# A hybrid attention block: the gate of GLA's second head before the second pair's queries and keys, its temporaries in other places, and pools of attention that wait tile by tile

## The chip, the cores and the metric

The kernel runs on one core of a Trainium2 chip, in one launch. The metric is the device time of one execution in microseconds (us). The kernel before takes 1225.82 us, the median of three runs (1225.39 to 1226.3).

## The reference

One encoder block over 1024 tokens (a grid of 16 rows and 64 columns) of width 1024, in float32. One normed input feeds one projection whose columns go to two kinds of attention heads: 8 heads of neighbourhood attention with a bias table, and 4 heads of gated linear attention (GLA), which is scanned in chunks of 64 tokens in both directions.

```python
n = rmsnorm(h, ln_g)
proj = n @ w_in
qa, ka, va, qg, kg, vg, rg, zf, zb = jnp.split(proj, offsets, axis=-1)
y_na = neighbourhood_attention(na_heads(qa), na_heads(ka), na_heads(va), rpb)
y_gla = bidirectional_gla(qg, kg, vg, rg, zf, zb, gu_f, gb_f, gu_b, gb_b, norm_g)
h = h + jnp.concatenate([y_na, y_gla], axis=-1) @ w_out
h = h + jnp.square(jax.nn.relu(rmsnorm(h, ln_ff_g) @ w_ff1)) @ w_ff2
return rmsnorm(h, ln_final_g)
```

Within GLA, per head and direction, with decay gates `log_a` from the low-rank factors z:

```python
b = jnp.cumsum(log_a.reshape(B, H, N, C, dk), axis=-2)
q_dec = q * jnp.exp(b)
k_inv = k * jnp.exp(-b)
A = jnp.where(mask, jnp.einsum('bhnid,bhnjd->bhnij', q_dec, k_inv), 0.0)
o_intra = jnp.einsum('bhnij,bhnje->bhnie', A, v)
contrib = jnp.einsum('bhncd,bhnce->bhnde', k * jnp.exp(b_last - b), v)
...
o = rmsnorm(o, norm_g) * jax.nn.silu(r)
```

## The kernel before

The work goes through stages: the x stage (load, norm, low-rank factors z, queries and keys of the first pair of heads; until about 44 us), GLA (to about 275), neighbourhood attention (to about 460), the output projection, the feed-forward part, and the final norm. The change touches the first three.

**Projections.** A projection takes one block of 128 columns of `w_in`. Float32 accuracy comes from two-part products: the normed input is kept as high and low part (nh, nl), the weights as wh and wl, and each of 8 steps along the width takes three matmuls (`product`, L198), so half a block (512 tokens) is 24 matmuls of 128x512. `proj` (L248) does two such halves, each into a PSUM buffer of the tag "mm", which has two: a half can start only when the half two before has been read out by its evacuation. The first stage's z sums use the same tag.

**Weights.** `weights` (L163) loads a block (wf, from SyncE's queue), makes wl by an ACT pass (L172) and a DMA of GpSimd that adds the block (L173), and wh by an ACT cast (L175). These ACT passes keep their program order. Two buffers of each: wf for the next block but one is sent for when wh of the block before is cast. The blocks follow the list `BLOCKS` (L48).

**Order of the work.** TensorE's instructions run in program order. On the other engines a scheduler orders them by priority, in which place in the program counts and `tc.high_priority(offset=...)` moves instructions up; each engine then works its list through strictly in order. GLA's own steps leave TensorE time, which generators fill: `Fill` (L122) steps through the projections of `FILL_ORDER` (L46): "v" values, "r" output gates, "q" queries and keys of the second pair of heads, "n" and "k" the first queries and keys of neighbourhood attention.

**Evacuations.** `qk_evac` (L267) scales half a projection of a pair of heads: for each of the two heads VectorE writes 64 rows (L278) and ACT copies them to the other 64 (L279). `z_evac` (L337) reads the z sums on VectorE (zf, L340), casts on ACT (zT, L341) and subtracts on VectorE (L342). `rstd_from` (L214) turns sums of squares to rms by Ln, Exp, Identity, Square on ACT and two VectorE passes; its temporaries are nt, nu and ny. `gla_v` (L449) reads values, `gla_r` (L466) an output gate: VectorE scales it (rm, L473), ACT takes Abs, Exp, Ln and Exp (L474 to L478), and VectorE finishes. Its temporaries rt and rm lie in the tags "g0" and "g1" of the pool "gla", two buffers each, which the norm of GLA, the decay gates (`gla_gates`, L497) and the values' temporaries use as well.

**GLA's steps for one head.** `gla_keys` (L519) forms kD, kI and qD; `gla_ktok` (L540) transposes kD (kt); `gla_contrib` (L555) sums states, ACT copies them (st, L568 and L571); `gla_scan` (L587) runs them through; `gla_within` (L573) makes the scores a, which VectorE masks into asb (L584); `gla_norm` (L611) norms and multiplies with yg (L617, L618).

**Start of attention.** The pools "na" and "qkv" open at L713 on memory that GLA's tiles had; a pool opened so waits until everything in that memory is done. Then the mask is loaded by GpSimd's queue (msk, L731) and the bias table of the first pair of heads by SyncE's (bt, L737); VectorE completes bt with msk (L742), and the softmax of the first block of scores sc reads it (L797).

Of the kernel before, what the change touches and what calls it, by code (L numbers as in the profile page):

```python
# [10 lines left out]
F32 = mybir.dt.float32  # L11
F32R = mybir.dt.float32r
U32 = mybir.dt.uint32
AF = mybir.ActivationFunctionType
ALU = mybir.AluOpType
# [3 lines left out]
P = 128  # L19
D = 1024  # L20
T = 1024
H = 512
# [22 lines left out]
)  # L45
FILL_ORDER = (('v', 0), ('r', 0), ('v', 1), ('q', 1), ('r', 1), ('v', 2), ('v', 3), ('r', 3), ('r', 2), ('n', 0), ('k', 0))  # L46

BLOCKS = (4, 8, 5, 1, 3, 9, 6, 7, 11, 10, 12, 16, 20, 13, 17, 21, 14, 18, 22, 15, 19, 23)  # L48
SOON = 200
SOON_W = 100  # L50
SOON_O = 100
SOON_V = 50
# [13 lines left out]
def block_kernel(ctx, tc, xT, g_mix, w_in, w_z, rpb, na_mask, gu, gb, g_gla, sel_f, sel_b,  # L66
                 rst, w_out, g_ff, w1, w2, g_fin, out):
    nc = tc.nc
    V, S, DMA, G = nc.vector, nc.scalar, nc.sync, nc.gpsimd

    L = "left"
    R = "right"
    pool = lambda name, side, bufs=1: tc.tile_pool(name=name, bufs=bufs, side=side)
# [89 lines left out]
    def weights(block, eng=None):  # L163


        with tc.high_priority(offset=SOON_W):
            wf = stg.tile([P, D], F32, tag="wf", name="wf")
            DMA.dma_start(wf, block)
            if eng is not None:
                return split(wf, eng)  # L170
            wl = stg.tile([P, D], F32R, tag="wl", name="wl")
            tc.keep_in_program_order(S.activation(wl, wf, AF.Copy, scale=-1.0))  # L172
            G.dma_start(wl, block, accum_op=ALU.add)  # L173
            wh = stg.tile([P, D], F32R, tag="wh", name="wh")
            tc.keep_in_program_order(S.copy(wh, wf))  # L175
            return wh, wl
# [3 lines left out]
    def block_parts(blk):  # L180

        if not parts:
            parts[blk] = weights(w_in[blk], G)
        n = BLOCKS.index(blk) + 1
        if n < len(BLOCKS):
            parts[BLOCKS[n]] = weights(w_in[BLOCKS[n]])
        return parts.pop(blk)
# [54 lines left out]
    rms = n_p.tile([P, T], F32, tag="rms", name="rms")  # L242
# [5 lines left out]
    def proj(blk, evac):  # L248

        w = block_parts(blk)  # L250
        for hf in range(2):
            d = bank("mm", f"proj{blk}_{hf}")
            yield from proj_part(d, w, hf * H, H)
            evac(hf, d)
# [5 lines left out]
    g0 = gla_stack.enter_context(pool("gla0", R))  # L260
# [6 lines left out]
    def qk_evac(g, which):  # L267

        dic, sc, t = ((qd, 0.125, "q"), (kd, 1.0, "k"))[which]
        for i in range(2):  # L270
            dic[2 * g + i] = (g0 if t == "q" and i else gk).tile([P, T], F32, tag={"k0": "k00", "q0": "k10", "k1": "k20"}.get(f"{t}{i}", "qd1"), name=f"{t}d{2*g+i}")

        def ev(hf, d):
            c = slice(hf * H, (hf + 1) * H)
            for i in range(2):
                dst = dic[2 * g + i]
                a, b = (slice(0, 64), slice(64, 128))[::1 - 2 * i]
                V.scalar_tensor_tensor(dst[a, c], d[a, :], sc, rms[a, c], op0=ALU.mult, op1=ALU.mult)  # L278
                S.copy(dst[b, c], dst[a, c])  # L279
        return ev  # L280

# [116 lines left out]
    def perm(t, hf):  # L398
        return t.rearrange("p (b r c) -> p b r c", b=NB, r=ROWS)[:, :, hf * 8:(hf + 1) * 8, :]

    def nat(d):
        return d.rearrange("p (r b c) -> p b r c", r=8, b=NB)

    def na_proj(p, nm, parts, tmp):

        def ev(hf, d):
            t = tmp()
            with tc.high_priority(offset=SOON):  # L410
                V.tensor_tensor(t, d, rms[:, hf * H:(hf + 1) * H], op=ALU.mult)
            x = [perm(x, hf) for x in parts]
            for i in range(2):
                own, other = slice(i * 64, i * 64 + 64), slice(64 - i * 64, 128 - i * 64)
                ti, hi = nat(t[own, :]), x[i][own]
                S.copy(hi, ti)
                if nm == "k":
                    S.copy(x[i][other], ti)
                lo, eng = (x[2][own], V) if nm == "k" else (x[i][other], G)
                eng.tensor_tensor(lo, ti, hi.bitcast(F32), op=ALU.subtract)  # L420
        return proj({"q": 12, "k": 16}[nm] + p, ev)


    yn_p = yg_pool.enter_context(pool("yn", L))
    q0 = [yn_p.tile([P, T], F32R, tag=f"yn{2 + i}", name=f"q0{i}") for i in range(2)]

# [17 lines left out]
    with pool("gla", R) as gp:  # L444
# [4 lines left out]
        def gla_v(h):  # L449
# [3 lines left out]
            def ev(hf, d):  # L453
                tmp = gp.tile([P, H], F32, tag="g1", name="vtmp", bufs=2)
                with tc.high_priority(offset=SOON):
                    V.tensor_tensor(tmp, d, rms[:, hf * H:(hf + 1) * H], op=ALU.mult)
# [9 lines left out]
        def gla_r(h):  # L466

            def ev(hf, d):
                c = slice(hf * H, (hf + 1) * H)
                t = gp.tile([P, H], F32, tag="g0", name="rt", bufs=2)  # L470
                m = gp.tile([P, H], F32, tag="g1", name="rm", bufs=2)
                with tc.high_priority(offset=SOON):
                    V.tensor_tensor(m, d, rms[:, c], op=ALU.mult)  # L473
                S.activation(t, m, AF.Abs)  # L474
                S.activation(t, t, AF.Exp, scale=-1.0)
                S.activation(t, t, AF.Ln, bias=1.0)
                V.scalar_tensor_tensor(t, m, 0.0, t, op0=ALU.min, op1=ALU.subtract)
                S.activation(t, t, AF.Exp)  # L478
                dst = t if (h, hf) in normed else yg[h][:, c]
                V.scalar_tensor_tensor(dst, m, ggla[:, 0:1], t, op0=ALU.mult, op1=ALU.mult)  # L480
                if (h, hf) in normed:
                    V.tensor_tensor(yg[h][:, c], yg[h][:, c], t, op=ALU.mult)
                else:
                    gated.add((h, hf))
            return proj(8 + h, ev)
# [137 lines left out]
                yield from proj(blk, qk_evac(g, which))  # L623

        def first_q(_):
            return na_proj(0, "q", q0, lambda: gp.tile([P, H], F32, tag="g1", name="qt", bufs=2))

        def first_k(_):

# [5 lines left out]

        for kind, i in FILL_ORDER:
            gen = {"v": gla_v, "r": gla_r, "q": gla_qk, "n": first_q, "k": first_k}[kind](i)
            fill.add(gen, (kind, i))
# [40 lines left out]
    yn = [yn_q.tile([P, T], F32, tag=f"yn{h}", name=f"yn{h}") for h in range(2)]  # L679
# [30 lines left out]
        with tc.high_priority(offset=SOON_O):  # L710
            V.tensor_tensor(hT[:, d, c], hT[:, d, c], o, op=ALU.add)

    with pool("na", L) as ap, pool("qkv", L) as qp:  # L713


        ap.tile([P, 2, 3], F32, tag="sm", name="sm", bufs=4)
        msk, bt0, pt0 = None, None, {}
        for tag in ("pt00", "pt01", "x", "msk", "pt10", "pad", "bt", "pt11", "vhl"):
            if tag == "msk":
                msk = ap.tile([P, 4, P], F32, tag="msk", name="msk")  # L720
# [7 lines left out]
                vhl[0] = ap.tile([P, NB, 2, P], F32R, tag="vhl", name="vhl0")  # L728
            else:
                pt0[tag] = ap.tile([P, 3, 3, P], F32R, tag=tag, name=f"pt0{tag[2:]}")  # L730
        G.dma_start(msk, na_mask)  # L731

        def bias_for(p):


            bt = bt0 if p == 0 else ap.tile([P, 2, 7, P], F32, tag="bt", name=f"bt{p}")
            DMA.dma_start(bt[:, :, 0:3, :], rpb2[:, 2 * p:2 * p + 2, :, :])  # L737
            rows = msk[:, 3:4, :].to_broadcast([P, 2, P])
            for i in range(2):
                for o, src, m in ((3, 1, rows), (5, 0, rows), (0, 0, msk[:, 0:3, :])):  # L740
                    n = 3 if o == 0 else 2
                    V.scalar_tensor_tensor(bt[:, i, o:o + n, :], bt[:, i, src:src + n, :], 8.0, m,  # L742
                                           op0=ALU.mult, op1=ALU.add)
            return bt
# [7 lines left out]
        def na_v(p):  # L752
# [18 lines left out]
            def ev(hf, d):  # L771

                if not hf:
                    vT.append((gk if p % 2 else qp).tile([P, T], F32, tag=f"k2{1 - p % 2}", name=f"vT{p}"))
                with tc.high_priority(offset=SOON):
                    V.tensor_tensor(perm(vT[0], hf), nat(d), nat(rms[:, hf * H:(hf + 1) * H]), op=ALU.mult)
# [85 lines left out]
        qt = lambda: qp.tile([P, H], F32, tag="qt", name="qt", bufs=2)  # L862
        qk = qk_tiles(0)
        fill.add(na_v(0), ("v", 0))
        bt = bias_for(0)
        fill.run(NA_PRE)
        xs = softmax(0, 0, *qk, bt)
        for p in range(NH // 2):
# [11 lines left out]
            for b in range(NB):  # L880
# [5 lines left out]
                if b + 1 == NB and p + 1 < NH // 2:  # L886
                    fill.until(("k", p + 1))
                    qk, bt = nxt, bias_for(p + 1)
# [68 lines left out]
    for d in range(NK):  # L957
        o = bank(("t", "s", "o")[d % 3], f"opl_{d}")
        t = yhl[0][:, NK - 1]
# [327 lines left out]
    with tc.high_priority(offset=150):  # L1287
        for n in range(2):
            p, i = f1.order[n]
# [131 lines left out]
    for c0, n in ((H, H), (0, Q), (Q, Q)):  # L1421
        c = slice(c0, c0 + n)
# [108 lines left out]
```

## Time and profile before

| | |
|---|---|
| median of three runs | 1225.82 us |
| the profiled execution | 1222.21 us |
| its span, first to last instruction | 1220.4 us |
| granted TensorE clock, mean | 0.982 of full |
| busy: TensorE matmul, VectorE, ACT, GpSimd | 1162.6, 873.1, 665.8, 248.1 us |
| longest waits of TensorE | 9.0 us at 275.61, 5.0 us at 103.34, 3.7 us at 243.39, 3.3 us at 219.28 |

The profile is of one execution, 3.6 us shorter than the median of the runs. In its rows, a timeline row gives start and duration in us, engine, line of the kernel, operation, output and inputs with their shapes, a count, and in brackets the idle time ahead and what ended it. A row of waits gives who waited and for which instruction: total, times, longest. PE is TensorE, DVE is VectorE, POOL is GpSimd, SP is SyncE, and SPq its queue of DMA issues. L113 is the helper through which every matmul goes, so matmuls are told apart by their tiles. Equal rows that follow each other are put together, with the count behind the x.

### The profile page before, as it was taken

To read this page: it belongs to the slowest core of one execution; us is meant where nothing else is said; L and a number is where in the kernel's file an instruction comes from. 1 tells how busy PE (TensorE), PEld (TensorE's weight loads), DVE (VectorE), ACT (ScalarE), POOL (GpSimd) and SP (SyncE) were. 2 spreads that over 40 slices of the span, in tenths; PEclk is the share of its full clock that TensorE was granted. 3 is DMA by queue.
4 is the path that set the end of the run, shared out by engine and by line. 5 is a ranking of instruction groups with operands and counts; after the bars stand their busy time and mean duration, and the time that the engine had idled before them with its cause. 6 is when DMAs were issued, how large, how long until landed. Compare 5 with 4: busy or idle time off the path is not lost.

```text
span 1220.4 us, 15431 instructions
## 1 busy us (share of the span) xinstructions
PE 1162.6 (95%) x5632; PEld 952.0 (78%) x5632; DVE 873.1 (72%) x1558; ACT 665.8 (55%) x1222; POOL 248.1 (20%) x199
## 2 busy tenths in 40 slices
PE   8998899886999999998999999999999999999996
PEld 8876687664877878876778888888888888888775
DVE  8786768645768686575776885876858768587467
ACT  6756565743656675443643644536445364453664
POOL 5200000201111213441103140321403214032004
PEclk9999899998999999998999999999999999999998
DMA  7333131313223314330111211112111121111203
GB/s 232 80 93 78 35 70 35 69 35 91 51 67 83 70 59 178 104 137 1 40 64 35 70 53 52 52 53 70 52 54 51 52 69 52 56 49 52 70 1 138
DMA packets 40283, 84.03 MB, mean 69 GB/s; under 512 B 9264, under 2 KB 20656, under 8 KB 40208
## 3 DMA queue, kind: packets, MB, share of 16 engines
q1 hardware_dynamic: 36608, 71.11, 17.5%
q0 software_dynamic: 3456, 11.94, 5.6%
q8 instruction: 44, 0.72, 0.2%
q14 instruction: 31, 0.25, 0.1%
q10 hardware_dynamic: 144, 0.00, 0.0%
HBM read 78.85 MB, written 5.96 MB: 69 GB/s over the span
## 4 chain that ended last, share of the span: by engine, by line
PE 72%; DVE 15%; ACT 8%; issue 2%; DMA 1%; SPq 0%; POOL 0%; DVEq 0%; ACTq 0%
PE f L113 24%; PE u L113 21%; PE proj L113 12%; PE op L113 5%; PE sc L113 2%; PE no L113 2%; DVE st L592 1%; PE pt L118 1%; PE o L113 1%; DVE st L589 1%; DMA bt<-rpb 1%; DVE nf L934 1%; DVE pl L1004 1%; DVE asb L584 1%; PE ob L113 1%
## 5 line engine op out<-in xcount | busy, mean ns | idle before, releaser
L1026 ACT CAST ph<-A 128x512 fp32r<-128x512 f32 x166 | 103.0, 621 | 146.2 <-PE f L113 73.3
L1004 POOL TENSOR_TENSOR ul<-uB,uh 128x512 fp32r<-128x512 f32 x84 | 109.1, 1317 | 330.5 <-ACT uh L1039 216.3
L113 PE MATMUL proj<-nh,wh 128*128 128x512 f32 x352 | 152.3, 433 | 8.3 <-DVE qd L278 5.0
L113 PE MATMUL f<-uh,ph 128*128 128x512 f32 x400 | 155.9, 390 | 1.6 <-ACT u L1047 1.4
L113 PE MATMUL f<-ul,ph 128*128 128x512 f32 x400 | 155.7, 389 | 0.1
L113 PE MATMUL f<-uh,pl 128*128 128x512 f32 x400 | 155.7, 389 | 0.0
L1004 DVE TENSOR_TENSOR pl<-A,ph 128x512 fp32r<-128x512 f32 x166 | 112.7, 688 | 52.6 <-ACT ph L1026 52.6
L113 PE MATMUL proj<-nh,wl 128*128 128x512 f32 x352 | 140.1, 398 | 0.0
L113 PE MATMUL proj<-nl,wh 128*128 128x512 f32 x352 | 139.4, 396 | 0.0
L1186 DVE TENSOR_TENSOR hT<-hT,f 128x512 f32<-128x512 f32 x168 | 113.0, 686 | 19.9 <-PE f L113 19.9
L113 PE MATMUL u<-n,ph 128*128 128x512 f32 x288 | 90.2, 395 | 2.0 <-ACT ph L939 2.0
L113 PEld LDWEIGHTS f<-uh,ph 128*128 128x128 f32 x400 | 75.1, 188 | 17.9 <-ACT u L1047 1.8
L113 PEld LDWEIGHTS proj<-nh,wh 128*128 128x128 f32 x352 | 67.6, 192 | 27.4 <-issue 14.7
L113 PEld LDWEIGHTS f<-ul,ph 128*128 128x128 f32 x400 | 75.1, 188 | 16.0 <-DVE ul L1004 0.4
L113 PEld LDWEIGHTS f<-uh,pl 128*128 128x128 f32 x400 | 75.1, 188 | 15.6
L1039 ACT CAST uh<-uB 128x512 fp32r<-128x512 f32 x84 | 51.9, 618 | 51.3 <-PE f L113 34.5
L113 PE MATMUL u<-T,ph 128*128 128x512 f32 x256 | 79.2, 391 | 0.1
L113 PEld LDWEIGHTS proj<-nh,wl 128*128 128x128 f32 x352 | 67.1, 191 | 15.3
L113 PE MATMUL op<-y,wh 128*128 128x512 f32 x240 | 77.0, 402 | 0.4 <-DVE y L693 0.4
L113 PEld LDWEIGHTS proj<-nl,wh 128*128 128x128 f32 x352 | 67.9, 193 | 11.9 <-issue 1.7
L173 POOL DMA_DIRECT2D wl<-in_w_in x21 | 18.1, 864 | 257.9 <-ACT wl L172 223.7
L799 ACT ACTIVATE xsc<-xsc,sm 128x384 f32<-128x384 f32 (+1 forms) x64 | 37.3, 584 | 58.5 <-DVE sm L797 58.0
(300 smaller groups left out, 2557.1 us busy)
## 6 DMA issues: line engine op xcount, KB each, us to landing
A<-in_w SPq DMA_DIRECT2D x64, 512.0 KB
wf<-in_w_in SPq DMA_DIRECT2D x22, 512.0 KB
wl<-in_w_in POOLq DMA_DIRECT2D x21, 512.0 KB, 6.9
wf<-in_w_out SPq DMA_DIRECT2D x17, 512.0 KB
hT<-in_xT SPq DMA_DIRECT2D x2, 2048.0 KB
xs<-in_xT SPq DMA_DIRECT2D x6, 512.0 KB
out<-hT SPq DMA_DIRECT2D x4, 512.0 KB
out<-hT SPq DMA_DIRECT2D x8, 256.0 KB
```

The lines of the kernel that those rows point to most:

```text
L113: m = nc.tensor.matmul(*args, **kw)
L118: tc.keep_in_program_order(nc.tensor.transpose(*args, **kw))
L173: G.dma_start(wl, block, accum_op=ALU.add)
L584: V.copy_predicated(asb[hf], sel.bitcast(U32).to_broadcast([P, 4, P]), src.rearrange("p (a b) -> p a b", a=4))
L589: V.scalar_tensor_tensor(st[0:64, i + 1, :], st[0:64, i, :], dec[0:64, i:i + 1], st[0:64, i + 1, :], op0=ALU.mult, op1=ALU.add)
L592: V.scalar_tensor_tensor(st[64:128, j - 1, :], st[64:128, j, :], dec[64:128, j:j + 1], st[64:128, j - 1, :], op0=ALU.mult, op1=ALU.add)
L799: S.activation(x[:, :n], x[:, :n], AF.Exp, scale=-1.0, bias=sm[:, i, 0:1], accum_out=sm[:, i, 1:2])
L934: V.scalar_tensor_tensor(dst, hT[:, d, hf * H:(hf + 1) * H], gff[:, d:d + 1], r, op0=ALU.mult, op1=ALU.mult)
L1004: return kp(eng.tensor_tensor(l, x, h.bitcast(F32), op=ALU.subtract))
L1026: kp(S.copy(ph, x))
L1039: kp(S.copy(uh, x))
L1186: kp(V.tensor_tensor(hT[:, d, c], hT[:, d, c], o[:, s], op=ALU.add))
```

## The change

It has four parts. The output gate of the second head (r1, block 9) moves ahead of the queries and keys of the second pair (blocks 1 and 3), in the fill order and in the list of weights. The VectorE half of `qk_evac` gets a raised priority, for both pairs. The gate's two temporaries become one tile rtm, in the two places yn2 and yn3, one for each half; these are the places of the first attention queries q0, which are therefore allocated later, in the generator that makes them. And the pools "na" and "qkv" wait tile by tile for the memory that they take over, while the mask's load and the first bias table get a raised priority.

```diff
-FILL_ORDER = (('v', 0), ('r', 0), ('v', 1), ('q', 1), ('r', 1), ('v', 2), ('v', 3), ('r', 3), ('r', 2), ('n', 0), ('k', 0))
+FILL_ORDER = (('v', 0), ('r', 0), ('v', 1), ('r', 1), ('q', 1), ('v', 2), ('v', 3), ('r', 3), ('r', 2), ('n', 0), ('k', 0))
-BLOCKS = (4, 8, 5, 1, 3, 9, 6, 7, 11, 10, 12, 16, 20, 13, 17, 21, 14, 18, 22, 15, 19, 23)
+BLOCKS = (4, 8, 5, 9, 1, 3, 6, 7, 11, 10, 12, 16, 20, 13, 17, 21, 14, 18, 22, 15, 19, 23)
 SOON = 200
+SOON_B = 300
...
-                V.scalar_tensor_tensor(dst[a, c], d[a, :], sc, rms[a, c], op0=ALU.mult, op1=ALU.mult)
+                with tc.high_priority(offset=SOON):
+                    V.scalar_tensor_tensor(dst[a, c], d[a, :], sc, rms[a, c], op0=ALU.mult, op1=ALU.mult)
                 S.copy(dst[b, c], dst[a, c])
...
-    q0 = [yn_p.tile([P, T], F32R, tag=f"yn{2 + i}", name=f"q0{i}") for i in range(2)]
+    q0 = []
...
-                t = gp.tile([P, H], F32, tag="g0", name="rt", bufs=2)
-                m = gp.tile([P, H], F32, tag="g1", name="rm", bufs=2)
+                tm = yn_p.tile([P, 2, H], F32, tag=f"yn{2 + hf}", name="rtm")
+                t, m = tm[:, 0, :], tm[:, 1, :]
...
         def first_q(_):
-            return na_proj(0, "q", q0, lambda: gp.tile([P, H], F32, tag="g1", name="qt", bufs=2))
+            q0.extend(yn_p.tile([P, T], F32R, tag=f"yn{2 + i}", name=f"q0{i}") for i in range(2))
+            yield from na_proj(0, "q", q0, lambda: gp.tile([P, H], F32, tag="g1", name="qt", bufs=2))
...
-    with pool("na", L) as ap, pool("qkv", L) as qp:
+    soon = lambda name: tc.tile_pool(name=name, bufs=1, side=L, reuse_waits="tile")
+    with soon("na") as ap, soon("qkv") as qp:
...
-        G.dma_start(msk, na_mask)
+        with tc.high_priority(offset=SOON_B):
+            G.dma_start(msk, na_mask)
...
-        bt = bias_for(0)
+        with tc.high_priority(offset=SOON_B):
+            bt = bias_for(0)
```

Lines after the edits are numbered one to six higher than before. VectorE's order at the end of the x stage, before; `z_354` are the z sums of the second half, `sb` and `ob` the sums of the first pair's queries and keys:

```order
L228 TENSOR_TENSOR nt<-nt,nu 128x256
L229 SCALAR_TENSOR_TENSOR rms<-nt,rms 128x256
L340 TENSOR_TENSOR zf<-z_354,rms 64x512
L278 SCALAR_TENSOR_TENSOR qd_157<-sb_371,rms 64x512
L278 SCALAR_TENSOR_TENSOR qd_158<-sb_371,rms 64x512
L342 TENSOR_TENSOR zT<-zf,zT 64x512
L278 SCALAR_TENSOR_TENSOR kd_159<-ob_528,rms 64x512
L278 SCALAR_TENSOR_TENSOR kd_160<-ob_528,rms 64x512
```

And after:

```order
L229 TENSOR_TENSOR nt<-nt,nu 128x256
L230 SCALAR_TENSOR_TENSOR rms<-nt,rms 128x256
L280 SCALAR_TENSOR_TENSOR qd_157<-sb_371,rms 64x512
L280 SCALAR_TENSOR_TENSOR qd_158<-sb_371,rms 64x512
L280 SCALAR_TENSOR_TENSOR kd_159<-ob_528,rms 64x512
L280 SCALAR_TENSOR_TENSOR kd_160<-ob_528,rms 64x512
L342 TENSOR_TENSOR zf<-z_354,rms 64x512
L344 TENSOR_TENSOR zT<-zf,zT 64x512
```

All four evacuations of the first pair stand ahead of zf now. On ACT at the same place, before (wl and wh are the passes over the next block's weights; rms, nt those of the last quarter's norm):

```order
L219 ACTIVATE nt<-ssq,small 128x256
L226 ACTIVATE nu<-ssq,small 128x256
L220 ACTIVATE rms<-nt,small 128x256
L227 ACTIVATE nt<-rms 128x256
L172 ACTIVATE wl<-wf 128x1024
L175 CAST wh<-wf 128x1024
L341 CAST zT<-zf 64x512
```

And after:

```order
L220 ACTIVATE nt<-ssq,small 128x256
L227 ACTIVATE nu<-ssq,small 128x256
L173 ACTIVATE wl<-wf 128x1024
L176 CAST wh<-wf 128x1024
L221 ACTIVATE rms<-nt,small 128x256
L228 ACTIVATE nt<-rms 128x256
L281 COPY qd_157<-qd_157 64x512
```

The weight passes stand ahead of the norm's Exp and Square now. VectorE in GLA, where the second head's keys are formed, before; `proj_0_970` and `proj_1_1047` are the two halves of the second pair's queries:

```order
L531 TENSOR_TENSOR kD_1152<-kD_1152,kd_160 128x1024
L278 SCALAR_TENSOR_TENSOR qd_961<-proj_1_1047,rms 64x512
L537 TENSOR_TENSOR qD_1161<-qD_1161,qd_158 128x1024
L278 SCALAR_TENSOR_TENSOR qd_962<-proj_0_970,rms 64x512
L278 SCALAR_TENSOR_TENSOR qd_962<-proj_1_1047,rms 64x512
```

And after, where `proj_1_1045` is the second half of gate r1 and `proj_0_1102` the first half of the queries:

```order
L482 SCALAR_TENSOR_TENSOR yg_101<-rtm,ggla 128x512
L537 TENSOR_TENSOR kI_1164<-kI_1164,kd_160 128x1024
L475 TENSOR_TENSOR rtm<-proj_1_1045,rms 128x512
L533 TENSOR_TENSOR kD_1154<-kD_1154,kd_160 128x1024
L539 TENSOR_TENSOR qD_1163<-qD_1163,qd_158 128x1024
L479 SCALAR_TENSOR_TENSOR rtm<-rtm 128x512
L482 SCALAR_TENSOR_TENSOR yg_101<-rtm,ggla 128x512
L280 SCALAR_TENSOR_TENSOR qd_1093<-proj_0_1102,rms 64x512
```

The gate's one pass has come ahead of kD and qD, and the queries' passes behind both. On SyncE's queue the first bias table stands behind the same loads of weights as before; the last of them is the one that goes out at 274.32.

## The prediction

> **What bounds the kernel now.** I read the engine line of the page first, then the list of what TensorE waited for, then the timelines of the engines around its three longest waits.
>
> ```profile
> PE 1162.6 (95%) x5632; PEld 952.0 (78%) x5632; DVE 873.1 (72%) x1558; ACT 665.8 (55%) x1222; POOL 248.1 (20%) x199
> ...
> PE sc L113 <- DVE sm L797: 9.0, 1, 9.0
> PE proj L113 <- DVE qd L278: 5.0, 1, 5.0
> PE a L113 <- DVE asb L584: 4.8, 3, 3.7
> PE proj L113 <- DVE rm L473: 3.3, 1, 3.3
> ```
>
> TensorE is busy for 95% of the span, and the change alters none of its matmuls, so only its idle time and its clock can move. The four rows under the page's line are its longest waits before the output projection (total, times, longest). Three of the four meet the change: 9.0 us ahead of the first attention scores, 5.0 us ahead of the key projection of the second pair, 3.3 us ahead of the first attention queries. The third (asb) stays as it is: the masks, the scan and what GpSimd does beside it are untouched.
>
> A long wait costs more than itself. This is the table of stretches; the column with a value between 0.5 and 1, behind the five busy times, is the granted clock:
>
> ```profile
> 108.00:113.00 5.00, 4.66 (x21) 4.12 (x22) 0.80 (x2) 3.22 (x4) 0.85 (x1) 0.66 0.17 24
> 224.00:229.00 5.00, 5.00 (x27) 4.05 (x26) 3.85 (x6) 4.97 (x9) 0.00 (x0) 1.00 0.01 3
> 247.00:252.00 5.00, 4.26 (x21) 3.50 (x22) 2.92 (x6) 0.00 (x0) 0.00 (x0) 0.66 0.71 150
> ```
>
> Behind the waits of 5.0 and 3.7 us the clock is 0.66 over 5 us, which loses 0.34 x 5 = 1.7 us of TensorE work; behind the 3.3 us it is 1.00 and nothing is lost.
>
> **Term A: the wait at 103 us goes.** VectorE and TensorE there:
>
> ```profile
> 104.52 1.23 DVE L531 TENSOR_TENSOR kD<-kD,kd 128x1024 f32<-128x1024 f32 x1
> 105.66 0.68 DVE L278 SCALAR_TENSOR_TENSOR qd<-proj,rms 64x512 f32<-64x512 f32 x1
> 106.26 1.21 DVE L537 TENSOR_TENSOR qD<-qD,qd 128x1024 f32<-128x1024 f32 x1
> 107.50 1.30 DVE L278 SCALAR_TENSOR_TENSOR qd<-proj,rms 64x512 f32<-64x512 f32 x2
> ...
> 102.96 0.39 PE L113 MATMUL proj<-nh,wl 128*128 128x512 f32 x1
> 108.34 0.75 PE L113 MATMUL proj<-nh,wh 128*128 128x512 f32 x1 [5.00 <-DVE qd L278]
> 119.04 0.39 PE L113 MATMUL proj<-nh,wh 128*128 128x512 f32 x1
> ```
>
> A half of a projection needs the PSUM buffer of the half two before it. The second pair's queries free theirs only with both evacuations of line 278. The second of them writes into the place of a first-pair tile that qD (106.26) still reads, so it runs at 107.50 and TensorE stands. After the change the gate r1 takes this turn. Its evacuation (L473) needs one pass of 0.69 us and writes into places of its own; it is queued ahead of kD and qD, so the bank is free by about 105. Nothing waits at 103. The gain is 5.0 + 1.7 for the clock = 6.7 us, and up to 0.8 more that TensorE loses until 119: at full rate 24 matmuls at the step of 0.23 us (102.96 is one of them) and some 2.7 us of GLA's make 8.2 us from 103.3, an end near 111.5 where the trace has the next half at 119.04. So 7.5 at most.
>
> Part of that is given back, since TensorE then comes earlier to work that other engines still owe it:
>
> ```profile
> 122.45 1.04 PE L118 MATMUL kt<-ident,kD 128*128 128x128 f32 x8
> 132.89 0.48 PE L113 MATMUL a<-qD,kI 64*128 64x128 f32 x2 [0.62 <-ACT st L571]
> 133.99 1.16 PE L113 MATMUL a<-qD,kI 64*128 64x128 f32 x14 [0.61 <-ACT st L571]
> 145.41 0.50 PE L113 MATMUL la<-zT,guh 128*128 128x512 f32 x1 [1.58 <-DVE asb L584]
> ...
> 118.25 0.69 ACT L226 ACTIVATE nu<-ov,small 128x512 f32<-128x512 f32 x1
> 138.89 0.63 ACT L474 ACTIVATE rt<-rm 128x512 f32<-128x512 f32 x1 [4.95 <-DVE rm L473]
> ```
>
> The transposes kt are 4 + 4, and the second four need the PSUM bank that ACT's Identity pass of the norm (nu, 118.25 + 0.69 = 118.9) empties. TensorE came at 122.45; 7.5 earlier it is at 114.95, at the second four by 115.4. The pass moves up by less, for the gate's activations, 0.63 each (138.89), stand among ACT's norm passes now: walked through in ACT's new order it ends near 117.0. So 1.6 us are lost. The scores a wait on ACT's state copies (L571), which take 0.6 us now twice; with TensorE earlier by 6 us and the copies earlier by less I get 2.8 instead of 1.2: another 1.6. Against this the 1.58 of la is covered, 1.4 of it. So A = 7.5 - 1.6 - 1.6 + 1.4 = 5.7 us. Bounds: 4 (the extra 0.8 absent, the copies one 1.0 us ACT pass later) to 7.5.
>
> **Term B: the wait at 219 us goes.** VectorE, then ACT behind it:
>
> ```profile
> 220.98 0.69 DVE L228 TENSOR_TENSOR nt<-nt,nu 128x512 f32<-128x512 f32 x1 [1.51 <-ACT nt L227]
> 221.77 0.69 DVE L473 TENSOR_TENSOR rm<-proj,rms 128x512 f32<-128x512 f32 x1
> ...
> 228.12 1.04 ACT L172 ACTIVATE wl<-wf 128x1024 fp32r<-128x1024 f32 x1
> 229.07 1.03 ACT L175 CAST wh<-wf 128x1024 fp32r<-128x1024 f32 x1
> 230.89 0.58 ACT L568 COPY st<-c 64x512 f32<-64x512 f32 x1
> ```
>
> The rm of gate r2 shared its two buffers with the norm's nt, and could start only when nt was read (220.98 + 0.69); the projection had long been done. With places of its own it runs when its projection ends, near 214, and the 3.3 us go. But next the contributions c need ACT's state copies, with the two weight passes of 2.0 us in front of them: these don't move up by 3.3. I keep 2.2 of 3.3 (bounds 0 and 3.3).
>
> **Term C: the start of attention.** VectorE, SyncE's queue, GpSimd, ACT:
>
> ```profile
> 274.92 0.69 DVE L618 TENSOR_TENSOR yg<-ny,o 128x512 f32<-128x512 f32 x1
> 282.31 1.90 DVE L742 SCALAR_TENSOR_TENSOR bt<-bt,msk 128x256 f32<-128x256 f32 x5 [6.71 <-DMA bt<-rpb]
> ...
> 274.32 0.33 SPq L168 DMA_DIRECT2D wf<-in_w_in  x1
> 275.73 0.38 SPq L737 DMA_DIRECT2D bt<-rpb  x1
> ...
> 276.20 0.56 POOL L731 DMA_DIRECT2D msk<-in_na_mask  x1 [1.69 <-DVE yg L618]
> ...
> 273.26 1.03 ACT L175 CAST wh<-wf 128x1024 fp32r<-128x1024 f32 x1
> ```
>
> The 9.0 us wait is a load: the bias table bt was sent for at 275.73, when the last yg of GLA (274.92 + 0.69) released the whole pool, and it landed near 282. Tile-wise waits free bt from that. But SyncE's queue issues in order, and the load of weights wf stands ahead of bt still; it waits for ACT's cast (273.26 + 1.03 = 274.29) and goes out at 274.32. So bt goes at about 274.65, 1.1 us sooner, the mask 1.7 sooner behind GpSimd's own weight load. The engines of the DMA move wl, wf, bt and the mask then together, so landing moves up by less: C = 0.8, bounds 0 and 1.7. Most of the 9.0 us stays.
>
> **Term D: a new wait at 49 us.** The raised priority is inside the evacuation routine, so the first pair's four evacuations in the x stage get it too, and go ahead of zf. VectorE, ACT and TensorE before:
>
> ```profile
> 46.63 0.42 DVE L229 SCALAR_TENSOR_TENSOR rms<-nt,rms 128x256 f32<-128x256 f32 x1
> 47.16 0.68 DVE L340 TENSOR_TENSOR zf<-z,rms 64x512 f32<-64x512 f32 x1
> 47.76 1.40 DVE L278 SCALAR_TENSOR_TENSOR qd<-sb,rms 64x512 f32<-64x512 f32 x2
> 49.91 1.41 DVE L278 SCALAR_TENSOR_TENSOR kd<-ob,rms 64x512 f32<-64x512 f32 x2
> ...
> 45.72 0.42 ACT L227 ACTIVATE nt<-rms 128x256 f32<-128x256 f32 x1
> 46.04 1.05 ACT L172 ACTIVATE wl<-wf 128x1024 fp32r<-128x1024 f32 x1
> 46.99 1.03 ACT L175 CAST wh<-wf 128x1024 fp32r<-128x1024 f32 x1
> ...
> 48.98 0.39 PE L113 MATMUL proj<-nh,wh 128*128 128x512 f32 x1
> ```
>
> The matmul at 48.98 opens the second half of the first value projection, in the buffer that zf empties. zf ends at 47.84, 1.1 us ahead: hidden now. After, two things stand before zf. ACT has both weight passes (1.05 + 1.03) ahead of the last quarter's Exp and Square, and its copies and zT's cast a little later, so Square ends near 49.0 in place of 46.1 and rms near 49.9 in place of 47.05: 2.9 us. Then the four evacuations of line 278, 1.40 + 1.41 = 2.8 us, run before zf. So zf ends at 47.84 + 2.9 + 2.8 = 53.5, and TensorE waits 53.5 - 48.98 = 4.5 us. With a wait between 3.7 and 5.0 the clock rows above add 1.7: D = 6.2, bounds 4.5 and 6.2. It has no cover: TensorE holds no other work in its order there, and nothing else waits within the following 50 us that a late TensorE would fill.
>
> [...]
>
> **Edits without a term.** The first attention queries now take the places that rtm leaves, so ACT's first cast of them waits for gate r2's last pass; that pass stands ahead of the queries' own evacuation in VectorE's order, so nothing is added. The second pair's evacuations, 1.30 us for two, fall among the third head's gates and scan; TensorE's following half of 24 matmuls, 5.5 us, hides them, or else they return as part of A's loss.
>
> **The sum.** -5.7 - 2.2 - 0.8 + 6.2 = -2.5 us. The profiled execution took 1222.21 us (span 1220.4), the median of three is 1225.82, 3.6 above; I carry the difference over: profile near 1219.7, median 1225.8 - 2.5 = 1223.3. About 0.2%, 2.45 us, is what a measurement of this kernel tells from no change, so this stands on that edge. Ends: best -7.5 - 3.3 - 1.7 + 4.5 = -8.0 (1217.8), worst -4 + 6.2 = +2.2 (1228.0).
>
> **Rivals.**
> 1. ACT becomes the limit of GLA (slower). The gate's four activations per half, at 0.63 us some 5.0 us in both, lie between ACT's copies of states and transposes, on which TensorE waits already (0.62, 0.61). If all 5.0 land ahead of those, A falls from 7.5 to about 2.5, B to 0.5 by the same queue, C to 0: -3.0 + 6.2 = +3.2, 1229.0. It is slower from the point where A, B and C together keep under 3.7. For it: B's copies move up by less than the wait. Against: ACT is busy for 55% of the span, and idle for 4.95 us in one piece before 138.89. Chance 0.20.
> 2. The new wait doesn't lower the clock, as behind the 3.3 us at 219: D is 4.5, sum -4.2, 1221.6. [...] Chance 0.15.
> 3. The new wait does not come: zf is earlier than I walk it, or a later wait absorbs what TensorE loses there. Sum -8.7, 1217.1. Against: the order of VectorE and ACT is fixed. Chance 0.12.
> 4. bt is sent for well before 274 because the queue ahead of it is free sooner. Then most of the 6.71 us goes: -2.5 - 6 = 1217.3. Against: the row of wf at 274.32. Chance 0.07.
>
> My forecast keeps 0.46, which the 0.2% edge splits into 0.21 faster, 0.24 within and 0.01 slower. Faster: 0.21 + 0.12 (of rival 2's 0.15) + 0.12 + 0.07 = 0.52. Slower: 0.01 + 0.17 (of rival 1's 0.20) = 0.18. Within 0.2%: 0.24 + 0.03 + 0.03 = 0.30. The range 1217.0 to 1228.6 takes in all but rival 1's far end and the tails of 3 and 4.
>
> **What would show it.** Right: in the waits of TensorE no qd at 103 and no rm at 219; a new proj behind zf (L342 after) of 4 to 5 us near 49; sc still at 8 to 9 us; waits on ACT's st and nu larger by some 3 us in all. Wrong: no wait behind zf (then rival 3), waits on ACT of 8 us or more in GLA (rival 1), sc at 3 us or less (rival 4), or a granted clock of 1.00 from 54 to 57 (rival 2).

## The result, and the profile after

The changed kernel takes 1217.29 us (median of seven runs, 1216.55 to 1221.04), the kernel before 1225.14 us (seven runs, 1222.42 to 1226.3). The ratio is 0.9944, with an interval from 0.9930 to 0.9958: by this ratio, which is taken over all runs, 6.9 us less, between 5.1 and 8.6 (the two medians alone are 7.9 apart). It is faster, as forecast, by nearly three times the 2.5 us of the forecast, and only 0.3 us inside the low end of the range. The profiled execution of after took 1217.29 us too, its span 1215.5: only 4.9 us less than that of before, whose profile (1222.21) lies below all the seven runs. That difference between profile and median becomes a main point below.

The longest waits of TensorE after, in the first 560 us, to be read beside those of before:

```profile
PE sc L114 <- DVE sm L802: 8.9, 1, 8.9
PE a L114 <- DVE asb L586: 6.7, 5, 3.7
PE proj L114 <- DVE zf L342: 4.7, 1, 4.7
...
PE a L114 <- ACT st L573: 1.7, 2, 1.1
PE proj L114 <- DMA wl<-in_w_in: 1.5, 1, 1.5
```

The 5.0 behind qd and the 3.3 behind rm are gone. The new 4.7 behind zf is there, and a wait that the prediction did not have: 1.5 us on a load of wl. The scores wait as long as ever.

The end of the x stage after, on VectorE, ACT and TensorE:

```profile
49.17 0.43 DVE L229 TENSOR_TENSOR nt<-nt,nu 128x256 f32<-128x256 f32 x1 [3.70 <-ACT nt L228]
49.63 0.42 DVE L230 SCALAR_TENSOR_TENSOR rms<-nt,rms 128x256 f32<-128x256 f32 x1
50.16 1.41 DVE L280 SCALAR_TENSOR_TENSOR qd<-sb,rms 64x512 f32<-64x512 f32 x2
51.60 1.41 DVE L280 SCALAR_TENSOR_TENSOR kd<-ob,rms 64x512 f32<-64x512 f32 x2
53.04 0.68 DVE L342 TENSOR_TENSOR zf<-z,rms 64x512 f32<-64x512 f32 x1
...
46.29 1.06 ACT L173 ACTIVATE wl<-wf 128x1024 fp32r<-128x1024 f32 x1
47.24 1.04 ACT L176 CAST wh<-wf 128x1024 fp32r<-128x1024 f32 x1
48.18 0.51 ACT L221 ACTIVATE rms<-nt,small 128x256 f32<-128x256 f32 x1
48.72 0.42 ACT L228 ACTIVATE nt<-rms 128x256 f32<-128x256 f32 x1
...
53.87 0.47 PE L114 MATMUL proj<-nh,wh 128*128 128x512 f32 x1 [4.71 <-DVE zf L342]
```

zf ends at 53.72 where 53.5 was worked out. And these are two stretches of 5 us of the changed kernel, behind that wait and at the place where TensorE stood before:

```profile
54.00:59.00 5.00, 5.00 (x15) 3.94 (x16) 1.38 (x2) 1.05 (x3) 2.45 (x6) 0.66 0.29 89
103.00:108.00 5.00, 5.00 (x33) 4.44 (x32) 4.89 (x5) 2.83 (x6) 0.00 (x0) 1.00 0.01 3
```

At 103 TensorE works without a gap at full clock. The same matmul in both traces tells how the difference builds up (start in before, in after):

| matmul | before | after | difference |
|---|---|---|---|
| second half of the first values' projection | 48.98 | 53.87 | +4.9 |
| gate r0, first half | 55.23 | 61.90 | +6.7 |
| decay gates of the second head, last | 92.38 | 99.04 | +6.7 |
| contributions c of the second head, first | 124.80 | 124.82 | 0.0 |
| decay gates of the third head, second half | 145.41 | 144.95 | -0.5 |
| o of the second head, second half | 150.55 | 148.49 | -2.1 |
| gate r2, second half | 213.64 | 210.82 | -2.8 |
| transposes kt of the fourth head | 225.46 | 220.74 | -4.7 |
| second scores of attention | 284.61 | 280.64 | -4.0 |
| sum of squares ahead of the feed-forward part | 568.83 | 563.98 | -4.8 |

The loss comes first and is then made good more than twice over. The step of 1.6 us between 145 and 151 has no wait beside it: it is a stretch of half clock that one execution had (145.91 to 149.33 in before) and the other hadn't. The two steps of 0.7 and 0.8 behind 225 are mostly of this kind too: outside the wait of the scores, the first has 3.4 us at half clock in before and 6.8 in after, the second 11.1 in before and 9.3 in after.

### The profile page after: what moved, and what is told of

The parts are those of the page before. It is cut to its first block, busy times and chain, and to the rows that moved or that the text cites. A ratio compares the mean times of both kernels' runs of the same rounds, so it can differ in the third digit from the quotient of the medians.

```text
span 1215.5 us, 15429 instructions
## 1 busy us (share of the span) xinstructions
PE 1158.5 (95%) x5632; PEld 948.7 (78%) x5632; DVE 874.8 (72%) x1558; ACT 665.1 (55%) x1222; POOL 248.3 (20%) x199
## 4 chain that ended last, share of the span: by engine, by line
PE 71%; DVE 15%; ACT 8%; issue 3%; DMA 2%; SPq 0%; POOL 0%; DVEq 0%; ACTq 0%
PE f L114 24%; PE u L114 21%; PE proj L114 13%; PE op L114 5%; PE sc L114 2%; PE o L114 2%; PE no L114 2%; DVE st L594 1%; PE pt L119 1%; DVE st L591 1%; DVE nl L309 1%; DMA bt<-rpb 1%; DVE pl L1010 1%; DVE asb L586 1%; DVE nf L940 1%
## 5 line engine op out<-in xcount | busy, mean ns | idle before, releaser
L114 PEld LDWEIGHTS f<-uh,pl 128*128 128x128 f32 x400 | 75.1, 188 | 15.7
L114 PE MATMUL u<-nt,ph 128*128 128x512 f32 x224 | 68.9, 389 | 0.0
```

The costliest lines, as they stand in the source:

```text
L114: m = nc.tensor.matmul(*args, **kw)
```

## The experiments

The theory after the first comparison: D, the early wait, is a pure loss of some 6.5 us; A and B are gains of about that and of 2 us; C is nothing because the load (384 KB) shares the DMA engines with larger ones (wl and wf, 512 KB each; the busy share is 0.90 from 272 to 274 in after). The rivals: D is needed as cover, the gate's ACT passes eat A, the table could go out early.

**Priority for the second pair only** (second_pair_only), from the kernel after:

```diff
-                with tc.high_priority(offset=SOON):
+                with tc.high_priority(offset=SOON if g else 0):
                     V.scalar_tensor_tensor(dst[a, c], d[a, :], sc, rms[a, c], op0=ALU.mult, op1=ALU.mult)
```

> The changed kernel with the raised priority of the query and key evacuations kept for the second pair only; the first pair's evacuations stand behind zf again. Theory (the new wait at 49 us is a pure loss of 4.7 us and of 1.8 us by the half clock behind it): no wait behind zf, clock 1.00 from 54 to 58, and the whole 6.5 us come off, near 1210.8 us, 0.988 of before. Rival (the lost time was cover: VectorE and ACT got ahead by it, so the waits on state copies and masks in GLA were kept small by it): the wait at 49 goes but waits on ACT's st, on asb and on the norm's nu grow by 3 us or more, and the time is 1214 to 1217 us.

Measured: 1210.74 us, ratio 0.9886 to before (0.9874 to 0.9899). No wait is left behind zf, and none of the others in GLA grew against the kernel after:

```profile
PE sc L114 <- DVE sm L802: 9.0, 1, 9.0
PE a L114 <- DVE asb L586: 5.1, 4, 3.7
...
PE a L114 <- ACT st L573: 1.7, 2, 1.0
PE proj L114 <- DMA wl<-in_w_in: 1.3, 1, 1.3
```

So D was a pure loss, 6.6 us between the medians of the two kernels (7.1 by their ratios to before), and the cover rival falls.

**The priority alone** (priority_alone), from the kernel before:

```diff
-                V.scalar_tensor_tensor(dst[a, c], d[a, :], sc, rms[a, c], op0=ALU.mult, op1=ALU.mult)
+                with tc.high_priority(offset=SOON):
+                    V.scalar_tensor_tensor(dst[a, c], d[a, :], sc, rms[a, c], op0=ALU.mult, op1=ALU.mult)
```

> The kernel before with the raised priority of the query and key evacuations alone. Theory: the wait at 49 us of 4.5 to 5 us with its half clock appears, and the wait at 103 us stays at 5.0, since the second query half still has to wait for qD: slower by 6 to 7 us, near 1231.5 us, 1.005 of before. Rival (the priority also relieves the wait at 103, or TensorE's delay is made up there): the wait at 103 shrinks by as much as the new one costs, and the time is within 2 us of before.

Measured: 1232.68 us, ratio 1.0063 (1.0048 to 1.0078), 7.7 us slower. Both waits stand in its list, zf 4.7 and qd 5.0 us. The loss is 1 us over the 6.7 of D in the trace of after, and the clock fits that: behind the same 4.7 us it is 0.50 over a like stretch of 5 us that had 0.66 there.

```profile
53.00:58.00 5.00, 4.45 (x11) 3.55 (x12) 1.78 (x3) 0.96 (x2) 2.46 (x6) 0.50 0.45 130
```

**The order alone** (order_alone): the lines FILL_ORDER and BLOCKS of the diff, on the kernel before.

> The kernel before with the new order of blocks alone: gate r1 ahead of the second pair's queries and keys, its temporaries where they were. Theory: the 5.0 us wait at 103 us and the half clock behind it go, and of the waits on the state copies some 1 us comes back: faster by 6 to 8.5 us, near 1218 us, 0.994 of before; the 3.3 us wait at 219 stays. Rival (the gate's eight ACT passes become the limit there, the second term of the prediction): the waits on ACT's st and asb grow to 5 us or more and the gain stays under 4 us.

Measured: 1215.47 us, ratio 0.9924 (0.9912 to 0.9937), 9.3 us faster, more than the 6 to 8.5 expected. The wait at 103 is gone, and what other engines owe TensorE in this stretch is small:

```profile
PE proj L113 <- DVE rm L473: 3.3, 1, 3.3
...
PE a L113 <- ACT st L571: 1.4, 2, 0.8
```

The rival of the gate's ACT passes falls: st takes 1.4 us in place of 1.2, the norm's nu holds up the transposes kt for 0.55 us, and the 1.6 us before la have shrunk to 0.4. A is more than the wait of 5.0 and the 1.7 us of clock that the first profile shows.

**The gate's temporaries alone** (rtm_alone): the edits of `gla_r`, q0 and `first_q` on the kernel before.

> The kernel before with the gate's temporaries in yn2 and yn3 alone. Theory: the 3.3 us wait at 219 us goes, a wait of about 1.5 us on the load of wl takes its place, and about 2 us remain: near 1223 us, 0.998 of before; the wait at 103 stays. Rival (the load's wait belongs to the other edits, since TensorE arrives earlier with them): the full 3.3 us remain, near 1221.8 us.

Measured: 1220.07 us, ratio 0.9963 (0.9949 to 0.9977), 4.5 us faster, between 2.8 and 6.2. That is more than either expectation. The list of waits shows what I expected:

```profile
PE proj L113 <- DVE qd L278: 5.0, 1, 5.0
...
PE proj L113 <- DMA wl<-in_w_in: 1.3, 1, 1.3
```

The 3.3 us became 1.3 on the load of wl, so the wait itself is worth 2.0, and a wait of 0.5 before a norm (ov, near 211.5 in before) went too. The remaining 2 us I could not see in the first profile of before: there the clock behind the 3.3 us is 1.00. In other executions with the same wait it isn't, as before_again below shows.

**The pools alone** (pools_alone): the tile-wise pools and the two priorities of the mask and the table on the kernel before.

> The kernel before with the tile-wise pools and the raised priority of the mask's load and the first bias table alone. Theory (the table is still sent for behind wf, 1 us sooner, and its landing is set by the transfers of wl and wf that it shares the DMA with): the wait of the first scores stays at 8.9 to 9.1 us, the time within 1 us of before. Rival (the table goes out when its memory is free, near 250): the wait falls to 3 us or less and 6 us or more come off.

Measured: 1224.36 us, ratio 1.0000 (0.9991 to 1.0009): nothing. The scores wait 9.1 us. C is zero, to within 1.1 us.

**Mask and table from ACT's queue** (tables_on_act), from the kernel after:

```diff
-            G.dma_start(msk, na_mask)
+            S.dma_start(msk, na_mask)
...
-            DMA.dma_start(bt[:, :, 0:3, :], rpb2[:, 2 * p:2 * p + 2, :, :])
+            (DMA if p else S).dma_start(bt[:, :, 0:3, :], rpb2[:, 2 * p:2 * p + 2, :, :])
```

> The changed kernel with the mask and the first bias table sent for from ACT's queue instead of GpSimd's and SyncE's, where they go out ahead of the last weight pass, near 268.4. Theory (it was the place behind wl and wf that kept them late): the table lands near 273 to 274, the wait of the first scores falls from 8.9 to 4 to 5 us, with less half clock behind it, and 4 to 6 us come off the changed kernel: near 1212.5 us, 0.990 of before. Rival (the load itself takes 6 to 7 us wherever it stands, or wl and wf now come late): the wait stays above 7 us or a wait on wl of as much appears at the next projection, and the time is within 2 us of the changed kernel, 1217.3.

Measured: 1210.10 us, ratio 0.9879 (0.9866 to 0.9893): 7.2 us below the median of the changed kernel (8.0 by their ratios to before, which took 1224.25 in these runs), more than expected. In the kernel after, SyncE's queue and VectorE:

```profile
270.82 0.38 SPq L742 DMA_DIRECT2D bt<-rpb  x1
...
278.34 1.90 DVE L747 SCALAR_TENSOR_TENSOR bt<-bt,msk 128x256 f32<-128x256 f32 x5 [6.65 <-DMA bt<-rpb]
```

And in this kernel, ACT's queue, VectorE and TensorE:

```profile
268.92 0.45 ACTq L742 DMA_DIRECT2D bt<-rpb  x1
...
272.28 1.90 DVE L747 SCALAR_TENSOR_TENSOR bt<-bt,msk 128x256 f32<-128x256 f32 x5
...
274.58 0.45 PE L114 MATMUL sc<-k00p,q 128*128 128x384 f32 x1 [2.26 <-DVE sm L802]
```

Sent 1.9 us sooner, the table is used 6.1 us sooner: 7.5 us from issue to use behind wl and wf, at most 3.4 ahead of them. What remains of the wait, 2.3 us, is VectorE's own passes over bt and the first scores. No stretch of half clock follows it in this profile: VectorE's next pass over values (vT) starts 5.1 us behind the start of the scores (279.66 against 274.58), where both_mended below, with such a stretch, needs 6.7 (273.35 against 266.69).

**Both mendings** (both_mended): the two diffs above together.

> The changed kernel with both edits: raised priority for the second pair only, mask and first bias table from ACT's queue. Theory: both gains add, near 1206 us, 0.984 of before. Rival (one covers the other): no better than the better of the two.

Measured: 1202.68 us, ratio 0.9820 (0.9806 to 0.9834), the fastest of all kernels here: 14.6 us below the changed kernel. Both gains add (6.6 and 7.2 are 13.8), and it is 3 us better than the 1206 expected, because the second gain was.

**Whole pools again** (whole_pools): both mendings, but the pools "na" and "qkv" as in the kernel before.

> The kernel with both mendings, but its attention pools wait as a whole again, as in the kernel before. Theory (the tile-wise wait and the place in the queue are needed together): mask and table now go out from ACT's queue only after the last yg of GLA, some 3 us later than the 260.5 of the mended kernel, but still ahead of wl and wf, so the wait of the first scores is 5 to 6 us in place of 2.4, with a half clock of 1.7 us or more behind it: 4 to 5 us slower than the mended 1202.7, near 1207. Rival (only the place in the queue counts): wait 2.4 again and the time within 1 us of 1202.7.

Measured: 1208.18 us, ratio 0.9870 (0.9850 to 0.9891), 5.5 us slower than with both mendings. The table goes out later and TensorE waits longer. With both mendings, and then with whole pools again:

```profile
260.92 0.44 ACTq L742 DMA_DIRECT2D bt<-rpb  x1
...
PE sc L114 <- DVE sm L802: 2.8, 2, 2.4
```

```profile
264.70 0.39 ACTq L741 DMA_DIRECT2D bt<-rpb  x1
...
268.08 1.90 DVE L746 SCALAR_TENSOR_TENSOR bt<-bt,msk 128x256 f32<-128x256 f32 x5 [3.92 <-DMA bt<-rpb]
...
PE sc L114 <- DVE sm L801: 6.2, 1, 6.2
```

So the tile-wise wait is worth something once the table has a free place in a queue, and nothing before.

**The two kernels once more** (before_again, after_again), one profile of each.

> The kernel before, profiled once more, for its clock: if the stretch of half clock behind a wait depends on where the wait lies on the clock's grid of 3.4 us, the same 5.0 us wait near 103 is followed by another number of half-clock stretches (one in the first profile), and the times of the same kernel differ by 1.7 us for each. If it depends on the wait alone, it is again one, 3.4 us long.

The kernel before now took 1226.18 us. Its waits are those of the first profile (4.98 at 103.81, 3.33 before 225.57, 9.03 at 280.64). The clock isn't:

```profile
108.00:113.00 5.00, 4.20 (x14) 3.66 (x15) 1.26 (x2) 3.22 (x4) 0.85 (x1) 0.50 0.10 12
113.00:118.00 5.00, 5.00 (x16) 3.70 (x16) 0.00 (x0) 1.75 (x3) 0.40 (x2) 0.54 0.90 224
...
226.00:231.00 5.00, 5.00 (x21) 4.04 (x20) 3.85 (x7) 3.91 (x8) 0.00 (x0) 0.66 0.00 0
```

At the 5.0 us there are three stretches of 3.4 us at half clock, from 107.40 (still inside the wait) to 117.64, where the first profile has one, from 108.37; and behind the 3.3 us there is one, where the first has none. The five stretches of the first profile between 100 and 290 us begin at 108.37, 135.67, 145.91, 248.31 and 279.03, which is 8, 3, 30 and 9 times 3.41 us apart. The matmuls show it too: those of 512 columns follow each other at 0.43 us in these stretches and at 0.23 outside. The next half of the projection starts at 122.09 in place of 119.04, 2.6 us later when the start of the wait is set equal.

> The changed kernel, profiled once more: the waits of 4.7 us near 49 and 8.9 us at the scores are the same to 0.1 us, no wait at 103 and none behind rm at 219, and the stretches of half clock behind them are another number of steps of 3.4 us. If instead the time differs between executions because a wait differs, one of these is another.

The changed kernel took 1217.76 us. Its waits are the same: 4.71 at 48.93, 8.91 at the scores, 1.24 on wl. At the 4.7 us there are now two stretches of half clock (51.62 to 58.44) in place of one. The time is only 0.5 us from that of the first profile.

## Why the prediction was right, and where it fell short

Right in direction and in what happens at each of the four places; short by a factor of nearly three in size. Three of the four terms came out above their own upper bounds (only A clear of the noise), for one reason above all: what the clock loses behind a wait was read from one execution. Point by point:

**D, the new wait: right, its clock mis-sized.** 4.5 us were worked out, 4.7 came, for the two reasons given. With the clock 6.2 us were put down, which was also the upper bound; the two experiments give 6.6 and 7.7 us. The 1.7 for the clock holds for one stretch behind the wait, as in the first profile of after; the three other profiles with this wait have two. The statement that nothing later would make it good is confirmed by second_pair_only.

**A, the wait at 103: right that it goes, mis-sized at two places.** The step "five of them fall before 117; 1.6 us are lost" at kt failed: TensorE waits there not at all in the kernel after, and 0.55 us in order_alone. It was worked out for a TensorE that comes 7.5 us earlier, as if the 6.2 us of D, which lie ahead of it, were not there: in the kernel after TensorE comes to the second head's contributions at 124.82, in before at 124.80. So the four terms were not independent, and the sum treated them so. The step "2.8 instead of 1.2" at the scores a came out as 1.7, so the sign "waits on ACT's st and nu larger by some 3 us" did not come: it is half a us. One wait was overlooked, 1.9 us on asb at 139 in the kernel after (0.0 in before, but 1.32 in before_again). And the clock: "0.34 x 5 = 1.7 us" was read from one execution. In the five profiles that have this wait the half clock that it brings lasts one, two or three stretches of 3.4 us: 3.4 (before), 6.8 (pools_alone), 10.2 (before_again, rtm_alone, priority_alone). Its cost goes from 1.7 in the first to some 4.6 us in rtm_alone, where the next half of the projection starts 18.6 us behind the wait's beginning in place of 15.7. Alone A measures 9.3 us, where the prediction kept 5.7 and bounded it by 7.5.

**B, the wait at 219: right that it goes, mis-sized.** "I keep 2.2 of 3.3": in the traces 1.9 to 2.1 remain, and 0.5 of the norm's wait in rtm_alone, but what takes the rest back is not the weight passes ahead of the state copies. It is the load of wl for this projection: in the kernel after it is sent for at 211.24, when ACT's pass for it has ended (209.90 + 1.04), TensorE comes for it at 216.88 and gets it at 218.33. That is 1.2 to 1.5 in the profiles with this edit. The step that failed is the reading of the row 224.00:229.00, "it is 1.00 and nothing is lost". Of the four other profiles with this wait, before_again and order_alone have 0.66 behind it, pools_alone and priority_alone 0.50; the rows are of order_alone and of pools_alone:

```profile
214.00:219.00 5.00, 5.00 (x21) 3.96 (x20) 3.84 (x7) 3.92 (x8) 0.00 (x0) 0.66 0.00 0
```

```profile
223.00:228.00 5.00, 5.00 (x12) 3.94 (x13) 3.85 (x7) 3.92 (x7) 0.00 (x0) 0.50 0.00 0
```

The first profile was the exception, and the clock behind the wait costs 1.7 us where it is one stretch (order_alone, before_again) and some 2.8 where it is two, the first 1.3 us of which lie inside the wait (pools_alone, priority_alone). Alone B measures 4.5 us, above its bound of 3.3.

**C, the table: right that most of the 9.0 stays, and why.** 0.8 was put down, zero measured, which was the lower bound: the issue did move up by 1.0 us against the last yg, and wl and wf ahead of it took that back. In the kernel after they go out at 269.72 and 270.39, bt at 270.82, and from 272 to 278 the DMA engines are busy for 0.90, 1.02 and 0.86 of each 2 us. Rival 4 fell with it in the kernel as changed; tables_on_act shows that its gain, 7 us, is there for another queue.

**The rivals.** The gate's ACT passes as the limit (slower) fell by order_alone. The wait that does not come (rival 3) fell by the 4.7 us behind zf; its 1217.1, like the 1217.3 of rival 4, is almost the time measured, so the time alone would have spoken for the wrong mechanism. The missing half clock behind the new wait fell: it is there in both profiles of after (0.66 from 54 to 59 in the first, 6.8 us at half clock in the second), in priority_alone (0.50 from 53 to 58) and in tables_on_act, where the last norm pass of ACT ahead of the mask's load comes 8.0 us later than in both_mended (268.46 against 260.46), 3.3 more than the wait of 4.7. The wait of 3.33 us, shorter than that, is followed by half clock in four profiles of five as well. In pools_alone the half clock sets in only 2.1 us after the 5.0 us wait has begun (at 103.48), and of the 3.41 us ahead of it TensorE was busy for 1.30. TensorE alone, its clock and the DMA in the two stretches:

```profile
102.18:105.59 3.41, 1.30 (x6) 1.00 0.01 2
105.59:109.00 3.41, 0.53 (x1) 0.50 0.00 0
```

The stretches in GLA last 3.41, 6.83 or 10.24 us, and in the five profiles they set in 2.1 to 5.0 us after the same wait has begun.

**The sum.** With the parts measured alone it is +7.7 - 9.3 - 4.5 + 0.0 = -6.1 us, inside the interval of the -6.9 measured. Without D the same sum is -13.8, and second_pair_only, which is the change without D, measures -14.0. That leaves nothing visible for the raised priority at the second pair, which no run has alone. That the time fell inside the range is partly luck: A and B were put 5.9 us too low, and D 1.5 too low and C 0.8 too high took 2.3 of that back. The trace pair of before and after, -4.9, is short of both because the first profile of before was a lucky one: 1222.21 us against 1224 to 1226 of most runs. The prediction stood on it.

What stays open: why the half clock behind the same 5.0 us lasts one stretch in one execution and three in another. Where it begins, 2.1 to 5.0 us behind the wait's start, differs by less than the 3.41 us whose multiples lie between the stretches of the first profile. For how long it lasts no reason was shown. Behind this wait come six matmuls of 512 columns and then sixteen small ones (o from qD and st, 64 columns). In before the six lie in the first stretch (108.37 to 111.78), and full clock follows. In before_again 1.4 us of the first stretch are still wait, the second is busy throughout but with the small ones, and full clock comes only after the third:

```profile
110.81:114.23 3.42, 3.42 (x17) 0.50 0.36 53
...
111.49 3.51 PE L113 MATMUL o<-qD,st 128*128 128x64 f32 x16
```

Whether the small matmuls have a part in it, no run tests.

## What to carry to other kernels

A priority raised inside a shared routine is raised for all its callers: here it cost 6.6 to 7.7 us at a caller where nothing was gained, and the order of instructions at each of them shows that before a run. A wait's price on TensorE is its length and the clock behind it, and the clock takes several executions to read: taking out waits of 3.3 and 5.0 us was worth 4.5 and 9.3. A delay put in early also undoes what later terms assume about when TensorE comes: add the terms up along the order of the program. The table's load, whose memory came free sooner, gained nothing here while larger transfers stood ahead of it; sent for ahead of them from another queue it gained 7.2 us, and 5.5 of the 14.6 with both mendings hang on its memory coming free sooner.

## What the runs showed of the hardware that was not expected

The half clock at a wait of 5.0 us lasted 3.4, 6.8 or 10.2 us in executions of the same kernel part, counted from where it sets in, which was inside the wait in four profiles of five. At the 8.9 to 9.2 us before the scores it was 10.2 us long in each of the nine profiles that have that wait, 6.8 us at the 6.2 us in whole_pools, and with the wait cut to 2.4 us in both_mended a single stretch was left:

```profile
267.00:272.00 5.00, 4.63 (x16) 3.42 (x15) 4.15 (x17) 2.70 (x10) 0.00 (x0) 0.66 0.45 125
```

Even 2.4 us can thus be followed by half clock; the 2.3 us in tables_on_act were not. A table that took 7.5 us from issue to use behind 1 MB of weights took 3.4 ahead of them.
